# A weighted two-way sum on one core: the weights in three transfers of 128 rows instead of one long and two half-height ones

## The chip, the cores and the metric

The kernel runs on one core of a Trainium2 chip. The metric is device time in microseconds (us), the median of several runs of the whole program. Loads and stores are DMA transfers; they are issued from two queues, that of the SP engine and that of the ACT engine, and the core's 16 DMA engines carry both. The arithmetic runs on DVE (the vector engine) and, near the end, partly on ACT (the scalar engine).

## The reference

Each of 16 x 1024 tokens has two expert outputs of 512 numbers and two weights. The result is their weighted sum.

```python
batch, seq, hidden, n_experts, k = 16, 1024, 512, 8, 2
# expert_outputs: (batch, seq, k, hidden) float32, combine_weights: (batch, seq, k) float32
weights = combine_weights[..., np.newaxis]
return np.sum(expert_outputs * weights, axis=2).astype(np.float32)
```

So 67.1 MB are read as expert outputs, 0.13 MB as weights, and 33.6 MB are written.

## The kernel before

The 16384 tokens are spread over 128 partitions, 128 tokens to each (`per` = 128). They are worked through in ten tiles along the token axis, `TILES = [13, 13, 12, 13, 13, 13, 12, 13, 13, 13]` tokens per partition: tiles 0 to 9. A token is 4 KB of input in each partition (two experts of 512 float32), so a tile of 13 tokens is loaded as 128 rows of 53,248 bytes, one of 12 as 128 rows of 49,152 bytes, and its result is stored as 128 rows of half that length. The last 13 tokens of every partition (tile 9; `main` = 115 tokens lie before it) come from a region of their own in memory, which is why their weights cannot be in the same row as those of the first 115.

On chip there are four rooms for tiles (`ROOM`). Tiles 0 to 3 are loaded at once at the start, by five loads from the SP queue (`FIRST = [2, 11, 13, 12, 13]`: tile 0 in a load of 2 tokens, as 256 rows of 4,096 bytes, and one of 11 tokens, as rows of 45,056 bytes; then tiles 1, 2 and 3). Tile 4 takes the room of tile 0, tile 5 that of tile 1, and so on: load g+4 is issued by SP when the store of tile g has landed in memory. Below, "load 4" is the load of tile 4 and "store 0" the store of tile 0.

The weights stand in one array `wt` with 8 bytes per token and partition. They are loaded from the ACT queue (L112 to L114), behind a small store of zeros (16 rows of 512 bytes, L111, into places that later stores overwrite). Stores 0 to 6 go through this same ACT queue; the last two stores (tiles 7 and 8 together, then tile 9) go through the SP queue (L129).

The arithmetic of a tile is in `combine`. Tiles 0 to 7 (`WHOLE`): DVE multiplies both experts in place with the weights (L88) and adds the two halves (L97). Tile 8 (`MIXED`): ACT scales ten of the first expert's token rows (L92), DVE does the rest (L94, L96, L97). Tile 9: ACT (L102) and DVE (L103) work token by token. The code inserts the waits: a multiplication waits for its load and its weights, a store for its addition, a load for the store that frees its room. The transfers share a small set of completion counters, so an issue also waits until the counter's earlier user is done: load 4 uses the counter of the second weight transfer, store 2 that of the third.

Of the kernel before, what the change touches and what calls it, by code (L numbers as in the profile page):

```python
# [1 line left out]

# [4 lines left out]


@with_exitstack
def kernel(  # L10
    ctx: ExitStack,
    tc: tile.TileContext,
    expert_outputs: bass.AP,
    combine_weights: bass.AP,
    out: bass.AP,
):

    nc = tc.nc
    b, s, k, h = expert_outputs.shape
    assert k == 2
    n = b * s
    P = nc.NUM_PARTITIONS
    per = n // P
    assert per * P == n

    ROOM = [13, 13, 12, 13]
    ROOMS = len(ROOM)  # L30
    SITE = [sum(ROOM[:i]) for i in range(ROOMS)]
    TILES = [13, 13, 12, 13, 13, 13, 12, 13, 13, 13]
    FIRST = [2, 11, 13, 12, 13]
    STORES = [[0], [1], [2], [3], [4], [5], [6], [7, 8], [9]]
    WHOLE = [0, 1, 2, 3, 4, 5, 6, 7]
    MIXED = [8]
    ALONE = 3
    FREE = {9: 0}
    LAST = 13
    assert all(c <= ROOM[g % ROOMS] for g, c in enumerate(TILES))  # L40
    assert sum(TILES) == per and [g for st in STORES for g in st] == list(range(len(TILES)))
    main = per - LAST
    starts = [sum(TILES[:g]) for g in range(len(TILES))]

    def rows(x):

        first = x[0 : P * main, :].rearrange("(p t) f -> p t f", p=P)
        second = x[P * main : n, :].rearrange("(p t) f -> p t f", p=P)
        return lambda t, c: first[:, t : t + c, :] if t < main else second[:, t - main : t - main + c, :]

    flat = out.rearrange("b s h -> (b s) h")
    eo = rows(expert_outputs.rearrange("b s k h -> (b s) (k h)"))
    cw = rows(combine_weights.rearrange("b s k -> (b s) k"))
    o = rows(flat)

    dt = mybir.dt.float32
    mult = mybir.AluOpType.mult
    add = mybir.AluOpType.add
    copy = mybir.ActivationFunctionType.Copy

    pool = ctx.enter_context(tc.tile_pool(name="all", bufs=1))
    et = pool.tile([P, sum(ROOM), k * h], dt)
    halves = et.rearrange("p j (k h) -> p (j k) h", k=k)
    wt = pool.tile([P, per * k], dt)
    wk = wt.rearrange("p (t k) -> p t k", k=k)
    zt = pool.tile([16, 128], dt)
    warm = pool.tile([P, 1], dt)

    def place(t):
        g = max(g for g in range(len(TILES)) if starts[g] <= t)  # L70
        return SITE[g % ROOMS] + t - starts[g]

    def load(t, c, **kw):
        at = place(t)
        assert place(t + c - 1) == at + c - 1
        nc.sync.dma_start(out=et[:, at : at + c], in_=eo(t, c), **kw)  # L76

    def weights(q, t, c):
        q.dma_start(out=wk[:, t : t + c, :], in_=cw(t, c))

    def combine(g, base):
        at, c, t0 = SITE[g % ROOMS], TILES[g], starts[g]
        if g in WHOLE or g in MIXED:
            room = halves[:, k * at : k * (at + c), :]
            x0, x1 = et[:, at : at + c, 0:h], et[:, at : at + c, h : 2 * h]
            if g in WHOLE:
                wb = wt[:, k * t0 : k * (t0 + c)].unsqueeze(2).to_broadcast([P, k * c, h])
                nc.vector.tensor_tensor(out=room, in0=room, in1=wb, op=mult)  # L88
            else:
                for i in range(ALONE, c):  # L90
                    x = et[:, at + i, 0:h]
                    nc.scalar.activation(out=x, in_=x, func=copy, scale=wt[:, k * (t0 + i) : k * (t0 + i) + 1])  # L92
                w1 = wk[:, t0 : t0 + c, 1:2].to_broadcast([P, c, h])
                nc.vector.tensor_tensor(out=x1, in0=x1, in1=w1, op=mult)  # L94
                w0 = wk[:, t0 : t0 + ALONE, 0:1].to_broadcast([P, ALONE, h])
                nc.vector.tensor_tensor(out=x0[:, 0:ALONE], in0=x0[:, 0:ALONE], in1=w0, op=mult)  # L96
            nc.vector.tensor_tensor(out=halves[:, base : base + c, :], in0=x0, in1=x1, op=add)  # L97
            return
        for i in range(c):
            t = k * (t0 + i)  # L100
            x0, x1 = halves[:, k * (at + i), :], halves[:, k * (at + i) + 1, :]
            nc.scalar.activation(out=x0, in_=x0, func=copy, scale=wt[:, t : t + 1])  # L102
            nc.vector.scalar_tensor_tensor(  # L103
                out=halves[:, base + i, :], in0=x1, scalar=wt[:, t + 1 : t + 2], in1=x0, op0=mult, op1=add
            )

    with tc.manual_schedule():
        nc.vector.memset(zt, 0.0)  # L108

        ahead = flat[0 : P * main, :].rearrange("(q t) h -> q (t h)", q=16)  # L110
        nc.scalar.dma_start(out=ahead[:, 0:128], in_=zt)  # L111
        weights(nc.scalar, 0, main)  # L112
        for half in (slice(0, P // 2), slice(P // 2, P)):
            nc.scalar.dma_start(out=wk[half, main:per, :], in_=cw(main, per - main)[half])  # L114
        nc.scalar.activation(out=warm, in_=nc.const_aps.tensor(1.0, (P, 1), dt), func=copy)  # L115

        t = 0
        for i, c in enumerate(FIRST):
            load(t, c, **({"max_dma_last_dim": k * h * 4} if i == 0 else {}))
            t += c  # L120
        assert t == sum(TILES[:ROOMS])
        for j, st in enumerate(STORES):
            room = FREE.get(st[0], st[0] % ROOMS)
            base, c = SITE[room] * k, 0
            for g in st:
                combine(g, base + c)
                c += TILES[g]
            assert c <= k * ROOM[room]
            q = nc.sync if j in (7, 8) else nc.scalar  # L129
            q.dma_start(out=o(starts[st[0]], c), in_=halves[:, base : base + c, :])  # L130
            for g in st:
                if g + ROOMS < len(TILES):
                    load(starts[g + ROOMS], TILES[g + ROOMS])


# [1 line left out]
_INS = ['expert_outputs', 'combine_weights']  # L137
_OUTS = [((16, 1024, 512), 'float32')]


# [23 lines left out]
```

## Time and profile before

| what | value |
|---|---|
| median of 3 timed runs | 238.83 us (238.82 to 238.92) |
| span of the profiled execution, first to last instruction | 237.1 us |
| the median over this span | 1.7 us |
| DVE busy | 190.0 us (80% of the span) |
| ACT busy | 15.8 us (7%) |
| moved by DMA | 100.80 MB in 3344 packets, mean 425 GB/s |
| share of the 16 DMA engines' span: SP queue, ACT queue | 75.9%, 23.0% |

The profiled execution has no time of its own beside its span here; what a run takes over the span is set at 1.7 us from the median and taken as unchanged. In the profile q1 is the queue of SP and q10 that of ACT. A packet is one row of a transfer (a run of contiguous bytes in one partition) or the 4-byte write with which each of the 16 DMA engines reports its part of a transfer done. "Landing" is when all 16 have reported. SPq and ACTq are the issuing sides of those engines.

### The profile page before, as it was taken

What the parts mean: (1) busy time and instruction counts of PE and PEld (TensorE: products, weight loads), DVE (VectorE), ACT (ScalarE), POOL (GpSimd) and SP (SyncE); (2) the same over time, 40 slices, a digit from 0 to 9 for tenths busy, and PEclk for the clock granted to TensorE, in tenths of its full rate; (3) what the DMA queues carried; (4) which work ended last, traced back from release to release, by engine and by line L of the source; (5) the groups of instructions that cost most, each with busy time, mean ns of one, the idle gap of its engine ahead of it and who ended that gap; (6) DMA issues with size and microseconds to landing.
All of it is one profiled execution on the core that took longest, in us unless ns stands there. A gap on an engine that the chain in (4) does not pass through costs nothing.

```text
span 237.1 us, 154 instructions
## 1 busy us (share of the span) xinstructions
DVE 190.0 (80%) x33; ACT 15.8 (7%) x25; POOL 0.2 (0%) x4
## 2 busy tenths in 40 slices
DVE  0006999999999999999999998998499969919400
ACT  2000000000000000000000000000000055019200
POOL 0000000000000000000000000000000000000000
DMA  8999999989999999999899999999899999899996
GB/s 300 388 481 434 432 421 398 470 348 485 449 431 458 431 440 390 486 420 420 359 492 409 409 509 392 431 503 431 359 431 503 420 397 483 381 431 431 431 431 287
DMA packets 3344, 100.80 MB, mean 425 GB/s; under 512 B 512, under 2 KB 656, under 8 KB 912
## 3 DMA queue, kind: packets, MB, share of 16 engines
q1 hardware_dynamic: 2000, 77.33, 75.9%
q10 hardware_dynamic: 1344, 23.47, 23.0%
HBM read 67.24 MB, written 33.56 MB: 425 GB/s over the span
## 4 chain that ended last, share of the span: by engine, by line
DVE 55%; DMA 36%; issue 1%; ACT 0%; DVEq 0%; ACTq 0%; SPq 0%
DVE et L88 35%; DVE et L97 17%; DMA out_dram<-et 17%; DMA et<-in_expert_outputs_dram 12%; DMA wt<-in_combine_weights_dram 8%; DVE et L103 3%; ACT et L102 0%; DVEq L159 0%; ACTq L111 0%; DVE zt L108 0%; DVEq L88 0%; SPq L76 0%; ACTq L102 0%
## 5 line engine op out<-in xcount | busy, mean ns | idle before, releaser
L88 DVE TENSOR_TENSOR et<-et,wt 128x13312 f32<-128x13312 f32 (+1 forms) x8 | 110.0, 13754 | 23.8 <-DMA wt<-in_combine_weights_dram 18.7
L97 DVE TENSOR_TENSOR et<-et 128x6656 f32<-128x6656 f32 (+1 forms) x9 | 62.8, 6973 | 0.4
L92 ACT ACTIVATE et<-et,wt 128x512 f32<-128x512 f32 x10 | 6.2, 708 | 188.0 <-DMA et<-in_expert_outputs_dram 188.0
L103 DVE SCALAR_TENSOR_TENSOR et<-et,wt 128x512 f32<-128x512 f32 x13 | 8.7, 747 | 5.0 <-ACT et L102 5.0
L102 ACT ACTIVATE et<-et,wt 128x512 f32<-128x512 f32 x13 | 8.1, 707 | 14.0 <-DMA et<-in_expert_outputs_dram 14.0
L94 DVE TENSOR_TENSOR et<-et,wt 128x6656 f32<-128x6656 f32 x1 | 7.1, 7093 | 2.3 <-DMA et<-in_expert_outputs_dram 2.3
L96 DVE TENSOR_TENSOR et<-et,wt 128x1536 f32<-128x1536 f32 x1 | 1.8, 1751 | 0.0
L115 ACT ACT_TABLE_LOAD x1 | 1.3, 1283 | 3.1 <-issue 3.1
L108 DVE MEMSET zt<- 16x128 f32 x1 | 0.2, 165 | 0.8 <-PEq L148 0.8
L115 ACT ACTIVATE warm<-const-float32-1.0 128x1 f32<-128x1 f32 x1 | 0.2, 203 | 0.0
L148 POOL MEMSET const-bfloat16-1.0<- 128x1 bf16 x1 | 0.1, 102 | 0.0
L148 POOL MEMSET const-uint8-127<- 128x1 uint8 x1 | 0.1, 101 | 0.0
L148 POOL MEMSET const-float32-0.0<- 128x1 f32 x1 | 0.1, 99 | 0.2 <-issue 0.2
L148 POOL MEMSET const-float32-1.0<- 128x1 f32 x1 | 0.1, 98 | 0.0
## 6 DMA issues: line engine op xcount, KB each, us to landing
et<-in_expert_outputs_dram SPq DMA_DIRECT2D x7, 6656.0 KB, 32.2
out_dram<-et ACTq DMA_DIRECT2D x5, 3328.0 KB, 34.7
et<-in_expert_outputs_dram SPq DMA_DIRECT2D x2, 6144.0 KB, 41.1
out_dram<-et SPq DMA_DIRECT2D x1, 6656.0 KB, 19.9
out_dram<-et ACTq DMA_DIRECT2D x2, 3072.0 KB, 37.2
et<-in_expert_outputs_dram SPq DMA_DIRECT2D x1, 5632.0 KB, 18.2
out_dram<-et SPq DMA_DIRECT2D x1, 3328.0 KB, 14.0
et<-in_expert_outputs_dram SPq DMA_DIRECT2D x1, 1024.0 KB, 5.0
```

The source lines that it names most:

```text
L88: nc.vector.tensor_tensor(out=room, in0=room, in1=wb, op=mult)
L92: nc.scalar.activation(out=x, in_=x, func=copy, scale=wt[:, k * (t0 + i) : k * (t0 + i) + 1])
L94: nc.vector.tensor_tensor(out=x1, in0=x1, in1=w1, op=mult)
L96: nc.vector.tensor_tensor(out=x0[:, 0:ALONE], in0=x0[:, 0:ALONE], in1=w0, op=mult)
L97: nc.vector.tensor_tensor(out=halves[:, base : base + c, :], in0=x0, in1=x1, op=add)
L102: nc.scalar.activation(out=x0, in_=x0, func=copy, scale=wt[:, t : t + 1])
L103: nc.vector.scalar_tensor_tensor(out=halves[:, base + i, :], in0=x1, scalar=wt[:, t + 1 : t + 2], in1=x0, op0=mult, op1=add)
L108: nc.vector.memset(zt, 0.0)
L115: nc.scalar.activation(out=warm, in_=nc.const_aps.tensor(1.0, (P, 1), dt), func=copy)
L148: nc = _bacc.Bacc("TRN2", target_bir_lowering=False, num_devices=1)
```

## The change

The number of weight transfers stays three, all from the ACT queue and in the same place. Before: all 128 partitions with 115 tokens (rows of 920 bytes), then for the last 13 tokens partitions 0 to 63 and partitions 64 to 127 (rows of 104 bytes). After: three transfers of all 128 partitions, of tokens 0 to 63 (tiles 0 to 4; rows of 512 bytes), 64 to 114 (tiles 5 to 8; 408 bytes) and 115 to 127 (tile 9; 104 bytes).

```diff
     starts = [sum(TILES[:g]) for g in range(len(TILES))]
+    SPANS = [0, starts[5], main, per]
...
         nc.scalar.dma_start(out=ahead[:, 0:128], in_=zt)
-        weights(nc.scalar, 0, main)
-        for half in (slice(0, P // 2), slice(P // 2, P)):
-            nc.scalar.dma_start(out=wk[half, main:per, :], in_=cw(main, per - main)[half])
+        for lo, hi in zip(SPANS, SPANS[1:]):
+            weights(nc.scalar, lo, hi - lo)
         nc.scalar.activation(out=warm, in_=nc.const_aps.tensor(1.0, (P, 1), dt), func=copy)
```

## The prediction

> **What bounds the kernel now.** I read the page first, for what is full. Its lines on the transfers (40 slices of the span; totals; the two queues' share of 16 DMA engines) then the first stretch of the table by stage (start:end, length, DVE, ACT and POOL busy, clock, share of the DMA engines in use, GB/s), then the waits of SP's queue (total, times, longest):
>
> ```profile
> span 237.1 us, 154 instructions
> DVE 190.0 (80%) x33; ACT 15.8 (7%) x25; POOL 0.2 (0%) x4
> DMA  8999999989999999999899999999899999899996
> DMA packets 3344, 100.80 MB, mean 425 GB/s; under 512 B 512, under 2 KB 656, under 8 KB 912
> q1 hardware_dynamic: 2000, 77.33, 75.9%
> q10 hardware_dynamic: 1344, 23.47, 23.0%
> 0.00:2.00 2.00, 0.17 (x1) 0.00 (x0) 0.20 (x4) 1.00 0.20 23
> SPq L76 <- DMA out_dram<-et: 152.6, 6, 38.4
> ```
>
> 75.9 + 23.0 = 98.9% of 237.1 us are 234.5 us of work for every DMA engine. Of the 2.6 us left, 0.8 x 2.0 = 1.6 us lie before 2 us; that leaves 1.0 us for all the rest, the end included. In between the engines hardly ever rest. DVE, the busiest of the others, is idle for 237.1 - 190.0 = 47 us: it is paced by loads, and the loads by stores that free rooms (SP waits 152.6 us for six of them). So the end moves only by added DMA work, by a stall inside a transfer, or by a new hole in the DMA traffic. The change must be priced in these three.
>
> **How the two queues share the DMA engines.** I asked the view of the transfers for three stretches: 6.4 to 18.4 us (rows of 45,056 against weight rows of 920 bytes), 19.5 to 34 (53,248 against 104) and 104 to 113 (53,248 against store rows of 24,576); and, last, 36.15 to 41.6, where SP's rows of 49,152 run alone. In pairs, SP's queue and ACT's; columns: packets, MB, share:
>
> ```profile
> q1 hardware_dynamic: 112, 5.05, 97.1%
> q10 hardware_dynamic: 112, 0.10, 2.5%
> ...
> q1 hardware_dynamic: 112, 5.96, 95.0%
> q10 hardware_dynamic: 112, 0.01, 0.6%
> ...
> q1 hardware_dynamic: 48, 2.56, 65.5%
> q10 hardware_dynamic: 48, 1.18, 30.4%
> ...
> q1 hardware_dynamic: 48, 2.36, 100.0%
> ```
>
> 112 against 112, and 48 against 48: the queues take turns, one packet each, whatever the length. A row's time is share x length x 16 / packets: 95.0% x 14.5 x 16 / 112 = 1.97 us for 53,248 bytes, 100.0% x 5.45 x 16 / 48 = 1.82 for 49,152, 2.5% x 12 x 16 / 112 = 0.043 us for 920 bytes, 0.6% x 14.5 x 16 / 112 = 0.012 us for 104. A weight row costs nearly nothing itself, but it waits a whole load row for its turn. The landings show it (the issues on ACT's queue by line, with their durations in ns and the times of the first and the last; below each, issue to landing):
>
> ```profile
> L79 ACTq DMA_DIRECT2D wt<-in_combine_weights_dram x1: 446/446/446, 1.4 to 1.4; - x1
> DMA to landing us min/median/max: 18.2/18.2/18.2
> ...
> L114 ACTq DMA_DIRECT2D wt<-in_combine_weights_dram x2: 510/561/612, 1.9 to 2.5; - x2
> ...
> DMA to landing us min/median/max: 27.4/31.0/34.6
> ```
>
> The first lands at 1.4 + 18.2 = 19.6 us. The first half lands at 1.9 + 27.4 = 29.3, 9.7 us later: 64 rows over 16 engines are 4 turns, the report of completion a fifth, 5 x 1.97 = 9.9. The second lands at 2.5 + 34.6 = 37.1.
>
> The Trainium skill ("DMA: Bandwidth & Descriptors", section Queues, rings and completion order) also has the engines go round the queues packet by packet, but with packets of typically 9 to 17 descriptors. By that a weight transfer would pass in one turn, and neither version could hold up a store. The equal counts above contradict it here: one row to a turn.
>
> **The change, part by part.** *DMA work.* Before, each engine moves 8 rows of 920 bytes and 4 + 4 of 104: 8 x 0.043 + 8 x 0.012 = 0.44 us. After, 8 rows each of 512, 408 and 104 bytes. On the straight line between the two measured lengths 512 bytes take 0.028 and 408 take 0.024 us: 8 x (0.028 + 0.024 + 0.012) = 0.51 us. The reports stay three. Added: **+0.07 us**, bounded by 0 and by 8 x 0.043 = 0.34 us (eight more rows at the longest row's time).
>
> *Issue.* Three issues on ACT's queue before and after, 0.45 + 2 x 0.56 = 1.6 us. Behind them ACT has only its warm-up until store 0 at 40.9 us, so even a doubling is covered. SP's queue is not touched.
>
> *The first multiplication.* Its wait, and the issue of SP's second load (tile 0's 11 tokens) and of its third (tile 1), the latter with its landing:
>
> ```profile
> DVE et L88 <- DMA wt<-in_combine_weights_dram: 18.7, 1, 18.7
> ...
> L76 SPq DMA_DIRECT2D et<-in_expert_outputs_dram x1: 461/461/461, 1.2 to 1.2; - x1
> ...
> L76 SPq DMA_DIRECT2D et<-in_expert_outputs_dram x1: 424/424/424, 1.7 to 1.7; - x1
> ...
> DMA to landing us min/median/max: 33.5/33.5/33.5
> ```
>
> It waits for load 0 too: the 11-token load takes 18.2 us from its issue at 1.2, as the weights do from 1.4, so it is there at 19.4 us, 0.2 us before them. The new first transfer has the same 8 turns with rows shorter by 0.015 us, so it lands 0.1 us earlier. 0.1 to 0.2 us for DVE, which is not what sets the end: 0.
>
> *New waits.* Tile 5's multiplication and tile 9's operations wait for the second and third transfer; so, through shared counters, do load 4 and store 2. The second lands near 35 us and the third near 50 (next step). Their users come at 67.8 us or later: 0.
>
> *The order of rows.* This is what really changes. Turns for weights: 9 + 5 + 5 = 19 before, 9 + 9 + 9 = 27 after. After, the second transfer's 9 turns go against load 1's 9, so it lands with load 1 at 1.7 + 33.5 = 35.2; the third's go against load 2's, and land near 35.2 + 8 x 1.83 = 49.9. Store 0 is issued at 40.9 into the same queue, behind it. The rows on that (issue of store 0, its landing, issues of store 1 and load 4, and SP's waits at the end for the last two stores):
>
> ```profile
> 40.91 0.34 ACTq L130 DMA_DIRECT2D out_dram<-et  x1
> DMA to landing us min/median/max: 26.8/26.8/26.8
> 61.97 0.34 ACTq L130 DMA_DIRECT2D out_dram<-et  x1
> 67.80 0.33 SPq L76 DMA_DIRECT2D et<-in_expert_outputs_dram  x1
> SPq L159 <- DMA out_dram<-et: 13.5, 2, 7.8
> ```
>
> Before, store 0 lands at 40.9 + 26.8 = 67.7 and SP, which has waited 38.4 us for it, issues load 4 at 67.8. After, store 0 begins when load 3 begins and they end together: 8 turns of 1.97 + 0.98 us (7.8 / 8, from the last store, which ends alone) make 23.6 us, so store 0 lands at about 73.5, **6 us later**, and load 4 is issued at 73.6, with SP's queue empty. What fills the DMA engines then is store 1, issued at 61.97: its 8 rows alone last 7.8 us, to about 81. Only a load 4 that takes over 7.5 us to its first row would leave a hole. For such a start the trace has two rows: the first load (issued at 0.73, first packets before 2 us) and store 0, whose queue was also empty while the other was full:
>
> ```profile
> 0.73 4.52 SPq L76 DMA_DIRECT2D et<-in_expert_outputs_dram  x5
> q1 hardware_dynamic: 11, 0.05, 40.1%
> ...
> DMA packets 0, 0.00 MB, mean 0 GB/s; under 512 B 0, under 2 KB 0, under 8 KB 0
> ...
> q1 hardware_dynamic: 16, 0.79, 73.4%
> q10 hardware_dynamic: 16, 0.43, 32.9%
> ```
>
> (In turn: 1 to 2 us; 43.9 to 45.7, where nothing starts; 43.4 to 46.4, with store 0's first row on each engine.) Store 0 is issued at 40.91 and starts after 45.7, 4.8 us; the first load needs under 1.3 us. Either way the row comes before 81: no hole, **0**, and the nearer row is store 0. The skill's page just named (Specifications) gives a first-byte latency of about 0.6 us for these queues; by that the sum is the same, while store 0's 4.8 us, part of it a wait for a turn, does not agree.
>
> *A stall.* Beside store 0's start the load row of 49,152 bytes took 73.4% x 3.0 = 2.20 us. Before it the same rows took 1.82. So the first store cost 0.38 us on each engine. After, it could fall away (the queue is no longer empty when store 0 comes) or come twice (load 4 joins a lone store): -0.38 to +0.38. I take 0, since one fresh mix of loads and stores happens in both.
>
> *Sum*: 237.1 + 0.07 = 237.2 us of span; with the 1.7 us around it, 238.83 + 0.07 = **238.9 us**, own range 238.5 to 239.3 (the stall's two ends).
>
> **The rivals.** *Slower: a hole before the last two stores.* The rows for it: who waits for loads 8 and 9, the issue of the store of tiles 7 and 8 and its landing, SP's queue from 212 to 228 us, and ACT's from 68.5 to 77:
>
> ```profile
> 192.62 6.23 ACT L92 ACTIVATE et<-et,wt 128x512 f32<-128x512 f32 x10 [188.03 <-DMA et<-in_expert_outputs_dram]
> 208.61 14.02 SPq L130 DMA_DIRECT2D out_dram<-et  x2
> DMA to landing us min/median/max: 19.9/19.9/19.9
> 212.80 8.07 ACT L102 ACTIVATE et<-et,wt 128x512 f32<-128x512 f32 x13 [13.95 <-DMA et<-in_expert_outputs_dram]
> ...
> q1 hardware_dynamic: 170, 7.16, 103.4%
> ...
> q10 hardware_dynamic: 64, 1.70, 46.4%
> ```
>
> The loads' place depends on how many rows of store 1 pass before load 4's first. Before, it was 4: from the end of store 0 to load 4's first row, 68.5 to 77 us, ACT's queue moved 64 packets, 4 for each engine. After, rows of 0.98 us pass alone from about 73.2 us, and load 4 joins at the end of a row after 73.6 + its delay: with the first load's 1.3 us the count is 2, with store 0's 4.8 less the load row that it may have had to let pass (2.8) it is 4, with the full 4.8 it is 6. Every row beyond 4 lets each later load land 0.98 us later. The tail pays for it. Load 8 lands at 192.6, and 16 us later the store of tiles 7 and 8 is issued, at 208.61. Load 9 ends near 212.4 (ACT sees it at 212.8), and that store's rows follow without a gap: it lands at 228.5, and 8 rows of 1.97 lead back to 212.4 (between 212 and 228 SP's queue is full). So 3.8 us are enough from issue to first row; whether 2 are, nothing shows. With 5 rows the issue slips to 209.6 while 212.4 stays, as all that goes before is the same work; the hole is 0 to 0.98 us, with 6 rows 0 to 2.0. It decides from the fifth row on. Near the upper end, at +0.8 with 5 rows, this gives 238.9 + 0.8 = 239.7 us, and with 6 at most 240.9. For it: store 0's slow start. Against it: the first load's quick one, and that a queue in service may take up new rows sooner. Fewer than 4 rows cost nothing: loads land earlier, stores later, the total stays.
>
> *Faster: weights of tile 0 to 4 earlier.* The largest single wait of DVE, 18.7 us, is for the weights, and the transfer that ends it gets shorter by half. But it is turns that it waits for, and load 0 ends only 0.2 us before. Even with the stall gone too, 238.9 - 0.38 - 0.2 = 238.3 us.
>
> *The change does not do what it says*: if store 0's rows were not kept behind the weights' rows, only +0.07 us is left, 238.9 again; it shares the forecast's time.
>
> **How the numbers follow.** A comparison of this kernel can tell about 0.2% (0.48 us) from no change. No hole and at most one stall either way (238.5 to 239.3): 0.54, "same". A hole of more than 0.4 us, or a smaller one on top of a second stall: 0.37, slower, likeliest 239.7. Faster by more than 0.48 us needs both gains in full: 0.09. Time 238.9, the forecast case's. The range reaches down to 238.5 (one stall gone) and up to 240.1 (a fifth row with its whole hole and half a stall); outside lie the larger holes and most of the faster case, some 0.2.
>
> **What would show it.** Right: the first weights land near 19.5, the second near 35, the third near 50; store 0 lands near 73.5 instead of 67.7 and load 4 is issued right behind it; packets 3472 (+128), the queues' shares still 234 to 235 us; the store of tiles 7 and 8 is issued within 1 us of 208.6 and lands near 228.5. Wrong: weights landing within a few microseconds of their issue (no turns); store 0 landing near 67.7; a slice below 8 near 74 or 212 us; load 8 landing past 193.5; a row time other than 1.97 and 0.98 us.

## The result and the profile after

| | us |
|---|---|
| before, median of 6 runs | 238.85 (238.81 to 239.01) |
| after, median of 6 runs | 240.34 (240.04 to 240.75) |
| ratio | 1.0064, 95% interval 1.0053 to 1.0075 |

The change makes the kernel slower by 1.5 us, 0.64%, and its runs scatter over 0.7 us where those of before keep within 0.2. The profiled execution took 240.75 us with a span of 239.0, so it is one of the slow ends of that range; 1.7 us lie outside the span, as before. In e1, in e17 and now and then in the kernel before, single runs near 241 us stand beside a median near 239; no profile shows one of them, and they widen the intervals of those ratios.

The page after, the lines that answer to those shown of before:

```profile
span 239.0 us, 154 instructions
DVE 190.2 (80%) x33; ACT 15.8 (7%) x25; POOL 0.2 (0%) x4
DMA  8999999989999989999999999989999999999995
DMA packets 3472, 100.80 MB, mean 422 GB/s; under 512 B 640, under 2 KB 784, under 8 KB 1040
q1 hardware_dynamic: 2000, 77.33, 75.7%
q10 hardware_dynamic: 1472, 23.47, 23.0%
```

The bytes are the same, there are 128 more packets, and no slice but the last falls below 8. But 98.7% of 239.0 us are 235.9 us of DMA work, 1.4 more than the 234.5 of before (the shares are rounded; the rows below account for 1.2), while the idle rest grows only from 2.6 to 3.1 us. For the most part the same rows have become longer. The landings of the weights and of store 0, and the issue of load 4 (the weights' transfers with their issue times and their landings; then store 0; then load 4):

```profile
L80 ACTq DMA_DIRECT2D wt<-in_combine_weights_dram x3: 446/453/694, 1.4 to 2.4; - x3
DMA to landing us min/median/max: 18.1/33.6/47.8
...
L130 ACTq DMA_DIRECT2D out_dram<-et x1: 351/351/351, 40.8 to 40.8; - x1
DMA to landing us min/median/max: 33.0/33.0/33.0
...
73.90 0.33 SPq L77 DMA_DIRECT2D et<-in_expert_outputs_dram  x1
```

The weights land at 19.5, 35.5 and 50.2 us, store 0 at 40.8 + 33.0 = 73.8 instead of 67.7, and load 4 is issued at 73.9. Then the view of the transfers: 73.4 to 78.2 us; the first long rows of load 4 (78.2 to 78.7, 78.7 to 79.5, both together as 78.2 to 80); the engines' second rows (81.5 to 83.5); and, of the kernel before, the first rows of load 4 (76.8 to 77.6):

```profile
q10 hardware_dynamic: 75, 2.00, 100.6%
...
q1 hardware_dynamic: 5, 0.27, 146.0%
...
q1 hardware_dynamic: 11, 0.59, 246.6%
...
q1 hardware_dynamic: 16, 0.85, 150.2%
...
q1 hardware_dynamic: 15, 0.80, 106.1%
...
q1 hardware_dynamic: 16, 0.85, 245.8%
```

Up to 78.2 us only ACT's queue runs: store 1, alone. Then 5 DMA engines take load 4 up, and the other 11 one store row later. A packet is counted where it starts, with its whole time: the first rows take 150.2% x 1.8 x 16 / 16 = 2.70 us, the second 106.1% x 2.0 x 16 / 15 = 2.26, where before the first take 245.8% x 0.8 = 1.97. Store 1's rows of that moment (76.9 to 78.2 us) are longer too:

```profile
q10 hardware_dynamic: 27, 0.72, 143.9%
```

143.9% x 1.3 x 16 / 27 = 1.11 us against 0.99. These rows start before any row of load 4 does, so the stall has begun before load 4's first row is counted. For each engine that is 0.73 (first row) + 0.28 (second) + 0.21 (store rows) = 1.2 us. And the engines are out of step from here on. At the end of load 9 (213 to 213.7 us, then 213.7 to 214.3; half of the packets are reports of completion, half first rows of the next store):

```profile
q1 hardware_dynamic: 30, 0.80, 265.4%
...
q1 hardware_dynamic: 2, 0.05, 20.6%
```

15 engines finish within 0.7 us and one later, which every landing must wait for: about 0.6 us more. With the 0.07 us of short rows this is the 1.9 us between the two spans. Load 8 is first used, and the store of tiles 7 and 8 is issued, 3.6 us later than before:

```profile
196.24 6.24 ACT L93 ACTIVATE et<-et,wt 128x512 f32<-128x512 f32 x10 [191.63 <-DMA et<-in_expert_outputs_dram]
...
212.23 12.25 SPq L130 DMA_DIRECT2D out_dram<-et  x2
```

Store 0's own start still costs too: the 16 load rows just ahead of its first row (they begin from 48.95 to 49.65 us) take 328.3% x 0.7 = 2.30 us instead of 1.97.

### The profile page after: what moved, and what is told of

It is laid out like the page before. It is cut to its first block, busy times and chain, and to the rows that moved or that the text cites. A ratio compares the mean times of both kernels' runs of the same rounds, so it can differ in the third digit from the quotient of the medians.

```text
span 239.0 us, 154 instructions
## 1 busy us (share of the span) xinstructions
DVE 190.2 (80%) x33; ACT 15.8 (7%) x25; POOL 0.2 (0%) x4
## 4 chain that ended last, share of the span: by engine, by line
DMA 63%; DVE 30%; ACT 0%; DVEq 0%; issue 0%; ACTq 0%; SPq 0%
DMA et<-in_expert_outputs_dram 28%; DMA out_dram<-et 27%; DVE et L89 18%; DVE et L98 9%; DMA wt<-in_combine_weights_dram 8%; DVE et L104 3%; ACT et L103 0%; DVEq L159 0%; ACTq L112 0%; DVE zt L109 0%; DVEq L89 0%; SPq L77 0%; ACTq L103 0%
```

## The experiments

The short rows need names: a turn is one packet of a queue, so a transfer of 128 rows takes 8 + 1 turns of each engine, one of 64 rows 4 + 1. "Spare" rows go into an array that nobody reads. In e3, e8 and the like, "load 4's first rows" are its first 16, one on each engine; 1.97 us is their time without a stall.

### Which part of the change costs

**e1: two transfers of 128 rows, 115 and 13 tokens (18 turns).**

```diff
-        for half in (slice(0, P // 2), slice(P // 2, P)):
-            nc.scalar.dma_start(out=wk[half, main:per, :], in_=cw(main, per - main)[half])
+        weights(nc.scalar, main, per - main)
```

> The weights in two transfers, 115 tokens and 13 tokens, both of 128 rows: 9 + 9 = 18 turns. Theory (the loss is a restart: the turns of the weights push store 0 until load 3 is over, SP's queue runs empty, and load 4 stalls as it starts beside a lone store): 18 turns are fewer than the 19 of before, store 0 lands near 67.7 us, no restart, 238.9 us. Rival (a third transfer of 128 short rows in place of the two halves is what costs): about half of the loss, 239.5 us or more.

Measured 238.95 us, ratio 0.9997 (0.9968 to 1.0026); load 4 issued at 67.96. Joining the two halves costs and brings nothing that this comparison can tell.

**e2: the kernel before, and 112 spare rows behind the weights (27 turns).**

```diff
+        nc.scalar.dma_start(out=spare[0:112, :]..., in_=cw(main, per - main)[0:112])
```

> The kernel before, with one transfer more on ACT's queue behind the weights: 112 rows of 104 bytes into a spare array that nobody reads, 7 + 1 turns, so 27 turns as in the changed kernel. Theory of the restart: store 0 lands near 73.5 us instead of 67.7, load 4's first row starts 4 to 5.5 us after its issue with a spread over the engines, and the time is that of the changed kernel, 240.0 to 240.8 us. Rival (the split of the first 115 tokens costs, not the number of turns): 238.9 us.

Measured 240.54 us, ratio 1.0069 (1.0054 to 1.0084). Load 4 is issued at 73.79 and its first rows (78.1 to 79.9 us) take 148.4% x 1.8 = 2.67 us:

```profile
73.79 0.33 SPq L77 DMA_DIRECT2D et<-in_expert_outputs_dram  x1
...
q1 hardware_dynamic: 16, 0.85, 148.4%
```

The weights of before with the changed kernel's number of turns have the changed kernel's loss. The split at 64 tokens and the shorter rows are not it.

**e4, e14, e10: the same with 64, 80 and 96 spare rows (24, 25 and 26 turns).**

> The kernel before with a transfer of 64 rows of 104 bytes more on ACT's queue, 4 + 1 turns, 24 in all. They end near 45.7 us, when store 0 starts anyway. Theory of the restart: nothing moves, 238.9 us; a loss begins only when the turns push store 0's rows. Rival (every turn of short rows costs): 5 of the 8 added turns, so over half of the loss, 239.7 us.

> The kernel before with 80 spare rows on ACT's queue, 5 + 1 turns, 25 in all, between 24 (238.9 us) and 26 (239.0 us). Both theories: load 4 is issued near 72 us, before or just as load 3 ends; 238.9 us.

> The kernel before with 96 spare rows on ACT's queue, 6 + 1 turns, 26 in all. Store 0 should land near 71.5 us while load 3 has one row left, and load 4 arrive some 3 us later: SP's queue is empty for one or two rows of store 1. Theory of a stall at every such gap: up to 240.3 us. Theory of the step: anything between 238.9 and 240.5, by whether the 16 engines take load 4 up after the same row.

Measured: 24 turns 238.89 us (ratio 1.0001, 0.9991 to 1.0010), load 4 issued at 69.84; 25 turns 239.37 us (1.0021, 1.0011 to 1.0030); 26 turns 238.97 us (0.9991, 0.9967 to 1.0015). With 24 store 0 begins one load row later (47.5 us against 45.7) and load 4 is issued 2 us later, and the time does not move. With 25 the run is 0.5 us slower, which neither theory expected. No row of load 4 is prolonged (98.3% x 2.0 = 1.97 us); 0.3 us of it stands at store 0's start, where the 16 load rows (47.2 to 47.8 us) take 410.9% x 0.6 = 2.47 us, against 2.20 before. The 26 turns are the surprise. Issue of load 4, ACT's queue alone (73.45 to 77.85 us), the first rows (77.7 to 79.5), how many begin from 77.8 to 78.4, and the later issue of the store of tiles 7 and 8:

```profile
73.82 0.33 SPq L77 DMA_DIRECT2D et<-in_expert_outputs_dram  x1
...
q10 hardware_dynamic: 64, 1.70, 89.7%
...
q1 hardware_dynamic: 16, 0.85, 109.5%
...
q1 hardware_dynamic: 16, 0.85, 328.5%
...
209.59 0.35 SPq L132 DMA_DIRECT2D out_dram<-et  x1
```

SP's queue is empty for 4.5 us (in e2 5.0), store 1 runs alone, and load 4 starts at nearly the same time. But all 16 engines take it up within 0.6 us, and its rows take 109.5% x 1.8 = 1.97 us. The gap alone costs nothing; the stall at its end does, and it can be absent.

**e17: the changed kernel, its third transfer on SP's queue behind the first load (18 turns left on ACT's).**

```diff
-        for lo, hi in zip(SPANS, SPANS[1:]):
+        for lo, hi in zip(SPANS[:-1], SPANS[1:-1]):
             weights(nc.scalar, lo, hi - lo)
...
             t += c
+            if i == 0:
+                weights(nc.sync, main, per - main)
```

> The changed kernel with its third weight transfer (13 tokens, 128 rows) issued on SP's queue, behind the first load of 2 tokens: 9 + 9 = 18 turns are left on ACT's queue. Theory (only the turns ahead of store 0 cost, through load 4's start beside a lone store): store 0 lands near 67.7 us, load 4 is issued at once while load 3 still runs, 238.9 us. Rival (three transfers of 128 rows cost in themselves): 239.5 us or more.

Measured 238.99 us, ratio 1.0025 (0.9994 to 1.0056), load 4 issued at 67.78. All three transfers of 128 rows are there, and in most runs the loss is not: six of the ten take 238.86 to 239.03 us. Three take 240.91 to 241.06, which no profile explains. So the turns ahead of store 0 are what brings the regular loss. In its profile the weights land 4.8, 9.5 and 23.5 us after their issue, the earliest far ahead of before, and the time does not follow, as tile 0 waits for its load.

### What the stall hangs on

**e3: the changed kernel, with 64 spare rows on SP's queue behind load 3.**

```diff
         assert t == sum(TILES[:ROOMS])
+        nc.sync.dma_start(out=spare[0:64, :]..., in_=cw(main, per - main)[0:64])
```

> The changed kernel, with 64 rows of 104 bytes into a spare array on SP's queue behind load 3: 4 + 1 turns, which keep this queue in service against 5 rows of store 1 until load 4 is there. The order of the long rows stays that of the changed kernel. If the stall comes from the queue that had run empty: it is gone, 238.9 to 239.1 us, load 8 lands within 1 us of 193.5, the 16 parts of a store land within 0.4 us of each other again. If it comes from reads that begin again beside a lone store stream, whatever the queue: 240.0 to 240.8 us as without the spare rows.

Measured 240.40 us, ratio 1.0072 (1.0056 to 1.0089); first rows (78.1 to 79.9 us):

```profile
q1 hardware_dynamic: 16, 0.85, 146.2%
```

2.63 us: the stall stays although short rows kept the queue in service, to 77.1 us. An empty queue is not its cause. Nor does an empty queue explain the long way from load 4's issue to its first row: issued at 73.78 into a queue in service, load 4 still starts at 78.16 at the earliest, and on 12 engines it lets one more row of store 1 pass.

**e6 and e11: the changed kernel with 128 spare rows behind the weights (36 turns), timed, then profiled once more.**

> The changed kernel with 128 rows of 104 bytes more on ACT's queue (into a spare array), 36 turns. Load 3 then ends near 65 us against short rows, store 0 runs alone and lands near 73, and load 4 begins near 78 beside store 1: no long row is read for 13 us instead of 5. Theory with one price for each restart: the same loss as the changed kernel, 240.0 to 240.8 us. Rival (the loss grows with the time without reads, or with the turns): 241.5 us or more.

> The kernel with 36 turns once more, for a second profile of it. Theory of the step: if this run is near 239.0 us, all 16 engines begin load 4 within one row of each other and its first rows take 1.97 us, as in its first profile; if it is near 240, they are split over two rows, and the first rows take 2.3 us and more. Rival: first rows of 2.3 us and more without a split, or a slow run without long rows.

Measured 239.80 us (239.04 to 240.17, ratio 1.0036, 1.0026 to 1.0045): nine turns more than the changed kernel and faster than it. Load 3 ends near 65 us and no long row is read for 12 us, so the loss does not grow with the gap. The first profile is of the fastest run, 239.04: load 4's first rows (77.7 to 79.5 us) take 1.97 us. The second took 240.07: 15 engines begin from 77.9 to 78.6, and one, which had started another store row, at 79.2 to 79.5:

```profile
q1 hardware_dynamic: 16, 0.85, 109.5%
...
q1 hardware_dynamic: 15, 0.80, 263.7%
q10 hardware_dynamic: 1, 0.03, 12.8%
...
q1 hardware_dynamic: 1, 0.05, 41.0%
```

In both profiles the rows take 1.97 us (263.7% x 0.7 x 16 / 15, and 41.0% x 0.3 x 16): neither has the stall, against the theory's 2.3 us and more for a slow run. What goes with the time in these two profiles is the engines' step: with one engine a row behind, for which all landings wait, the run takes 1 us more.

**e8, e12, e13, e9: the changed kernel with load 4 issued later.** GpSimd fills n elements of the freed room between the landing of store 0 and load 4's issue (n = 256, 500, 620, 768).

```diff
                 if g + ROOMS < len(TILES):
+                    if g == 0:
+                        nc.gpsimd.memset(et[:, SITE[0], 0:256], 0.0)
                     load(starts[g + ROOMS], TILES[g + ROOMS])
```

> The changed kernel; between the landing of store 0 and the issue of load 4 GpSimd fills 256 elements of the freed room with zeros (load 4 overwrites them), so that load 4 is issued some 0.4 us later, about half a row of store 1. Theory of the step: in the changed kernel load 4 reaches the DMA engines just as they pass from one row of store 1 to the next, so some take it up a row earlier than others (5 of 16 at 78.3, 11 at 79 us), and the stall belongs to this split. Half a row later all 16 take it up after the same row: no stall, 238.9 to 239.3 us, though load 4 starts later. Rival (reads that begin again beside a lone store stall in any case): 240.0 to 240.8 us or more.

> The changed kernel with 500 elements filled by GpSimd ahead of load 4: issue near 74.4 us, so that load 4 should reach the engines near 78.5, in the middle of a row of store 1. Theory (an arrival late in a row, with time left before the next, is free; one early in a row or at the passage costs the stall): part of the runs near 239, the first profile with little prolongation. Rival (every start beside a lone store costs about 1 us, the free ones were luck): 240.0 to 241.0 us as with the other delays.

> As the run before, with 620 elements: issue near 74.5 us, arrival near 78.6, late in a row of store 1, some 0.3 us ahead of the passage. Theory of the moment: all 16 engines take load 4 up at the passage at 78.9 to 79.2, rows of 1.97 us, 238.9 to 239.3 us. Rival (every start costs): 240.0 to 241.0 us.

> As the run before it, with 768 elements, so that load 4 comes later still, perhaps near the next passage from row to row. Theory of the step: if the engines are split again, the stall is back, 240 us and more; if all take it up after the same row, 238.9 to 239.3 us. Rival (a stall in any case): 240.0 to 240.8 us whatever the step.

| | load 4 issued at | median us | ratio (95%) |
|---|---|---|---|
| after | 73.90 | 240.34 | 1.0064 (1.0053 to 1.0075) |
| e8 | 74.12 | 240.81 | 1.0063 (1.0035 to 1.0092) |
| e12 | 74.36 | 240.47 | 1.0068 (1.0041 to 1.0095) |
| e13 | 74.46 | 240.56 | 1.0075 (1.0053 to 1.0098) |
| e9 | 74.64 | 240.62 | 1.0061 (1.0035 to 1.0086) |

In e8 all 16 engines take load 4 up within 0.6 us (78.7 to 79.3), and its first rows (78.7 to 80.5) still take 145.6% x 1.8 = 2.62 us (in e12, e13 and e9 2.52, 2.50 and 2.71):

```profile
q1 hardware_dynamic: 16, 0.85, 436.9%
...
q1 hardware_dynamic: 16, 0.85, 145.6%
```

So the theory of the step fell: engines in step can stall as well, and no later moment tried here is free. An earlier one, with 27 turns, was not tried.

**e15 and e16: the changed kernel with store 1 in two transfers, of 1 and 12 or 12 and 1 tokens.**

```diff
-            q.dma_start(out=o(starts[st[0]], c), in_=halves[:, base : base + c, :])
+            for lo, hi in ((0, 1), (1, c)) if j == 1 else ((0, c),):
+                q.dma_start(out=o(starts[st[0]] + lo, hi - lo), in_=halves[:, base + lo : base + hi, :])
```

> The changed kernel with store 1 in two transfers, of 1 and of 12 tokens (8 rows of 2,048 and 8 of 24,576 bytes for each engine). The passages from row to row then lie near 73.8 + 0.91 n, that is 77.4, 78.3 and 79.2 us, and load 4, issued near 73.9 as before, reaches the engines near 78.0, between two of them: all 16 take it up near 78.3, after five long rows, with three left. Theory (the boundary decides; five rows are free): 238.9 to 239.3 us. Rival (an arrival within a row costs, or the turns of the weights do): 240.0 to 240.8 us.

> The same with 12 tokens first and then 1: passages near 73.1 + 0.91 n, that is 77.7 and 78.6 us. Load 4 arrives near 78.0 and is taken up near 78.6 by all 16, after six rows of 0.91 us, with two and the short ones left. Theory (after the sixth row it stalls): 240 us and more. Rival (only a split of the engines stalls): 238.9 to 239.3 us.

Measured 240.63 us (1.0066, 1.0049 to 1.0083) and 240.39 us (1.0063, 1.0048 to 1.0078). In e15 load 4's rows begin from 78.2 us, most after five long rows as expected, and take 174.1% x 1.45 = 2.52 us (78.15 to 79.6):

```profile
q1 hardware_dynamic: 16, 0.85, 174.1%
```

In e16 six rows pass, and load 4's first rows take 2.48 us, as its theory had it. But e15 stalls after five, so the place of the boundary or the number of long rows does not decide it alone.

One regularity stands in the profiles, though no run was made to test it. Wherever load 4 starts beside a store 1 in one transfer, it is free when five of its rows or fewer have passed on all but one engine at most (four in the kernel before, five in e10, e6 and e11), and stalls when a sixth has passed on 11 engines or more (after, e2, e3, e8, e12, e13, e9). The rows of store 1 that start ahead of load 4 in e10 (72.9 to 77.85 us) and after (72.9 to 78.2), each with 16 reports of completion:

```profile
q10 hardware_dynamic: 96, 2.13, 99.9%
...
q10 hardware_dynamic: 107, 2.42, 109.9%
```

That is 80 rows, five for each engine, against 91. Among the starts beside a lone store 1, the free ones are also the early ones: first row at 78.03 us or before, against 78.16 or later. Count and moment are not told apart here, and e15, with eight short rows of store 1 ahead of the long ones, fits only the moment.

### Two that were to avoid it

**e5: the changed kernel with load 3 in two transfers, `FIRST = [2, 11, 13, 12, 6, 7]`.**

> The changed kernel with its three weight transfers as they are, but load 3 in two transfers, of 6 and of 7 tokens (rows of 24,576 and 28,672 bytes). Store 0's 8 rows then pass against the first of them, and store 0 lands near 65 us while the second is still under way, so that reads never stop. Theory (the loss is the stall of reads that begin again beside a lone store stream): no stall at load 4, 238.9 to 239.2 us although the weights take the same 27 turns. Rival (27 turns of weights, or rows of 512 and 408 bytes, cost in themselves): 240.0 to 240.8 us.

Measured 242.11 us (240.36 to 242.99, ratio 1.0149, 1.0130 to 1.0167), the worst of all. Store 0 does land near 65.8 us and reads go on. But all eight rows of store 1 now pass against the second part of load 3, ahead of load 4's first: loads 4 to 8 land later, and the store of tiles 7 and 8 is issued at 212.74. From 212.4 to 213.5 us SP's queue has 15 reports of completion and not one row:

```profile
212.74 10.43 SPq L130 DMA_DIRECT2D out_dram<-et  x2
...
q1 hardware_dynamic: 15, 0.00, 0.8%
```

This is the hole that the prediction's slower rival describes, about 1 us of it, in a kernel where loads fall further behind than in the changed one. The start of store 0 also costs more here than before (0.7 us for each engine against 0.4). The profile is of the fastest run, 240.36 us; what the other three lose beyond it is not shown. The stall at load 4 is gone, as expected: its first rows (81 to 82.5 us) take 131.7% x 1.5 = 1.97 us. But the time says little on the stall, since the edit moved the rows as well.

**e7: the kernel before, with a small store of 64 rows of zeros ahead of store 0.**

> The kernel before with a small store behind the weights: 64 rows of 512 bytes of zeros into places of tile 3 that store 3 overwrites, 4 + 1 turns, done before store 0 begins at 45.7 us. If the stall at store 0's start (0.39 us for each engine in the kernel before) belongs to the first writes into a fresh part of memory, it goes, and the time is 238.5 us. If it belongs to a long stream that joins another, it stays: 238.9 us.

Measured 238.96 us (1.0004, 0.9995 to 1.0013): the stall at store 0's start stays, with load rows that exceed their usual time by 0.5 us for each engine (0.4 before). None of the 17 experiments beats the kernel before.

## Why the prediction was wrong

- **Bound and turns: right.** DMA engines full from 2 us to the end; weights at 19.5, 35.5 and 50.2 us (forecast 19.5, 35, 50).
- **The order of rows: right.** Store 0 lands at 73.8 (73.5) and load 4 is issued at 73.90 (73.6) into an empty queue; store 1 fills the DMA engines; load 4 starts at 78.2 to 79.4, within the 4.8 us from the issue to the start of store 0 that the prediction called the nearer row, plus a row for most engines. Five rows of store 1 pass on 5 engines and six on 11, within the forecast's 2 to 6.
- **The stall: the step that failed.** It was priced from one start, that of store 0 among loads, at -0.38 to +0.38 us, and taken as 0 because "one fresh mix of loads and stores happens in both". Measured at load 4: 1.2 us on the mean engine, and up to another 0.6 on the slowest, on which every landing hangs. The count of one start in both was wrong too: in the kernel before load 4 follows load 3 in a queue that is never empty, and starts without a stall (1.97 us), while store 0's start costs 0.33 us after the change, nearly as before; load 4's comes on top. A load that starts among store rows is not the mirror image of a store that starts among load rows; and a mean over engines is no bound where all 16 must report. Of the prediction's signs of being wrong, a row time other than 1.97 and 0.98 us is this term, and load 8 past 193.5 us comes of it and of the rows of store 1 that pass. This term is the whole difference between the two spans but for the 0.07 us of short rows.
- **The slower rival: right in sign, wrong in mechanism.** Its chain is there: load 8 is used at 196.2 instead of 192.6, and the store of tiles 7 and 8 is issued at 212.23. But its price needed 2 to 3.8 us from that issue to the first row. The lines above show 15 engines passing from load 9 to that store from 213 to 213.7 us, 0.8 us after the issue, without a gap. So a hole opens some 3 us beyond the issue of before and not 1; e5 went that far. e10 shows it directly: five rows pass, the issue slips to 209.59 as the rival has it, and the time stays at 238.97. That the rival's bound for six rows, 240.9 us, covers the measured time is luck. The range, made with this rival at 240.1 us, ended 0.24 us below the median.
- **The faster rival: did not come.** Weights that are there earlier (e17) move no end.
- **What was shown and what stays open.** Shown: turns of short rows ahead of store 0 (e2 against e1, e4 and e17) empty SP's queue, and the loss is the stall as load 4 starts beside a lone store (the row times of after, e2 and e3 against e10). Shown not to be the cause by themselves: the length of the weight rows, the empty queue, the length of the gap, the split of the engines. Open is why the start is free with 26 turns, and in both profiles with 36, where with 27 it was not in any of nine (after, e2, e3, the four delays, e15, e16); five passed rows or fewer, or an early moment, go with the free ones.

The Trainium skill ("DMA: Bandwidth & Descriptors", section "Specifications") gives about 0.6 us from a transfer's issue to its first byte. In the changed kernel the store of tiles 7 and 8 comes near it (0.8 us from issue to first row) and load 4 does not (4.4 us).

The state of a transfer's own queue does not separate the two. In e3 SP's queue was in service until 77.1 us and load 4 took 4.4 us; in e5 the queue had emptied by 212.9 us, and the store issued at 212.74 began at 213.6, 0.9 us after. What differs here is the other queue: ACT's is busy with store 1 in the first case, and in the second, as at 212.23 us in the changed kernel, it has moved no row for 8 us or more. Load or store makes no such difference: store 0, in the kernel before, took 4.8 us beside a busy SP queue, and the first load, with nothing beside it, under 1.3.

## What to carry to other kernels

When two queues share the DMA engines by turns, count packets and not bytes: a few hundred bytes in short rows on each engine can hold back a store of megabytes behind them by as many long rows of the other queue, so short transfers go where no long one waits behind them. A saturated kernel can still lose time without any idle engine: look at the time of a row at each place where a stream starts again beside another, and at the slowest of the 16 engines, not at their mean. And a cost taken from a single start of a stream is a sample and no bound.

## What the runs showed that was not expected

- A load that starts among store rows can cost 0.9 to 1.2 us on each engine (first rows 2.5 to 2.7 us instead of 1.97) or nothing (e10), within 0.1 us of the same issue time (73.79 in e2, 73.82 in e10).
- From issue to first row it is 4.0 to 4.7 us for a load 4 that starts beside a lone store 1, and 0.8 to 0.9 us for the store of tiles 7 and 8 with ACT's queue idle (changed kernel and e5).
- Engines that fall out of step stay so: in the changed kernel one of 16 ends load 9 over 0.5 us behind the others, 135 us after the stall. That it is the engine that started load 4 last is not shown, as the rows do not name their engine.
